# One place more in a ring of raw weights, the residual's rows in a ring of three, and the parts of the output projection in a bound order

## The chip, the cores and the metric

One core of a Trainium2 chip runs the kernel; the other cores are idle. The metric is device time in microseconds (us) of one execution, smaller is better. A measurement's figure is the median of several executions.

## The reference

One layer of a hybrid encoder: 512 rows of `x` and 16 learned meta rows ahead of them, 1024 channels, float32. Two branches (stick-breaking attention and gated linear attention) are merged by gates, go through the output projection `w_o`, and are added to the input through a norm; then comes a gated MLP with a causal convolution. The part around the change is:

```python
mix = (gate_sb * (sb @ w_sb_out[l]) + gate_gla * (o @ w_gla_out[l])) @ w_o[l]
h = h + _rmsnorm(mix, norm_mix_post[l])
hn = _rmsnorm(h, norm_ffn_pre[l])
up = hn @ w_ffn_up[l]
act = gelu(_causal_dwconv(up, conv_w[l], conv_b[l]))
ffn = (act * (hn @ w_ffn_gate[l])) @ w_ffn_down[l]
h = h + _rmsnorm(ffn, norm_ffn_post[l])
return h[:, N_META:]
```

`_rmsnorm` divides each row by the root of its mean square and multiplies by a gain for each channel. `w_sb_out` has 512 rows, `w_o` 1024 x 1024, the up and gate weights 1024 x 2816.

## The kernel before

Products in float32 are made of three matmuls: each operand is split into a high part, rounded to the matmul's type (`h`), and the remainder (`l`), and high x high, high x low and low x high are summed in PSUM. A weight therefore goes through four places: a raw tile in a ring (`raw`, three places, `load_w`, L79), loaded by SyncE's DMA queue (SP); its rounded copy by ScalarE (`wh`, L88); its remainder by GpSimd (`wl`, L89); then TensorE. A raw place is free when both have read it. A framework decides from the code the order in which each engine gets its instructions; `tc.issue_after(x)` binds an instruction behind another one.

The stages by the profile's time: input norm to 20 us, linear attention to 250, stick-breaking and gates to 490, `w_sb_out` and the output projection to 570, the second norm and the first MLP tiles to 605, the MLP's up and gate products to 815, the down projection to the end. The down projection is made of seven products of half-size matrices; some of its operands are sums of two weight blocks, which GpSimd's DMA adds while loading (`tv`, L1115).

The stage of the change works on four tiles of 128 rows (i = 1 to 4) and the two halves of 512 output columns:

- `mix` (L795 to L811): the gated sum for each of eight groups of channels, split into `mh` and `ml`. `w_o`'s second half of columns is loaded into `woh` and `wol` here. For the 16 meta rows, `meta_products` adds small matmuls with the raw weights.
- `second(i)` (L925): the second half of columns for tile i, 24 matmuls of 128 x 512, into the PSUM tile `wob{i}`. `second(1)` and `second(2)` come early, `second(3)` and `second(4)` after the first halves. The dictionary `between` puts other work behind certain matmuls.
- `first_half(i, ks)` (L946): the first half of columns, also 24 matmuls a tile, from the weights `oa0` to `oa6`. Tiles 1 and 2 share one PSUM tile of two banks, `wo12`, tiles 3 and 4 share `wo34`. Groups 0 to 3 go round over all tiles, groups 4 to 7 tile after tile (12 matmuls each, bound behind the last `wob` matmul).
- `gained(i, pt, hf)` (L837): ScalarE sums the squares of a half (`wj`), VectorE multiplies it by the gain `g1bc` into `hb`. It is the last reader of the PSUM half.
- `normed(i)` (L853): the norm's factor (`mix`, `r_mix`, `a_mix`), VectorE's two operations that scale `hb` and add the residual rows `xr`, ScalarE's two squares (`wk`), the next factor (`ffn`, `r_ffn`, `a_ffn`), and two operations that make `y`.
- `turned(i, b)` (L869): four transposes of `y` on TensorE (`ht`) and their split into `h2h`, `h2l`, by ScalarE and VectorE.
- `mini` (L881): norm, residual and second norm of the meta rows, in small operations, from `mc`, a copy of the meta sums; TensorE's part is a packing of 64 small matmuls (`mini`) and two sums (`msmix`, `msffn`). It is a generator that stops twice, so its three steps can be put at three places.
- L967 loads the first two up weights, L976 the first two gate weights; L979 to L986 begin their products.

The residual's 512 rows (`xr`, 2 MB) and the broadcast gains `g1bc` and `g2bc` are loaded on ScalarE's queue at the stage's start (L829 to L833).

Of the kernel before, what the change touches and what calls it, by code (L numbers as in the profile page):

```python
# [9 lines left out]
F32 = mybir.dt.float32  # L10
# [6 lines left out]
P = 128  # L17
D = 1024
# [31 lines left out]
def block_kernel(ctx: ExitStack, tc: tile.TileContext, x, meta_tokens, norm_mix_pre, w_in, w_gk_up, b_gk,  # L50
# [3 lines left out]
    pe, act, dve, pool, sp = nc.tensor, nc.scalar, nc.vector, nc.gpsimd, nc.sync  # L54

    x = x[0]
# [8 lines left out]
    wp = ctx.enter_context(tc.tile_pool(name="wp", bufs=3))  # L65
# [13 lines left out]
    def load_w(src, nk, name, hi_out=None, lo_out=None, lo_eng=pool, into=None):  # L79

        ncol = src.shape[-1]
        raw = wp.tile([P, nk, ncol], F32, tag="raw", name=f"raw_{name}")
        sp.dma_start(raw, src)
        last_raw[0] = raw
        if hi_out is None:
            hi_out = (into or wp).tile([P, nk, ncol], F32R, tag="wh", name=f"wh_{name}", bufs=2)
            lo_out = (into or wp).tile([P, nk, ncol], F32R, tag="wl", name=f"wl_{name}", bufs=2)
        act.copy(hi_out, raw)  # L88
        lo_eng.tensor_tensor(out=lo_out, in0=raw, in1=f32(hi_out), op=ALU.subtract)  # L89
        return hi_out, lo_out  # L90
# [127 lines left out]
    with tc.tile_pool(name="p0", bufs=2, side="right") as p0:  # L218
# [37 lines left out]
        def turned(i, dr):  # L256
            if not i:
                tp = pst("tpm")
                last_tp[0] = pe.matmul(tp[:, :P], xm, dr, start=True, stop=True)
                split_g(p0, hnh[:, :, :NM], hnl[:, :, :NM], tp[:, :P].rearrange("p (t k) -> p k t", k=KT), gT, "m")  # L260
                return
            t = slice(NM + (i - 1) * P, NM + i * P)
            for b in range(2):
                tp = pst(f"tp{i}_{b}", "sz"[i % 2])
                for k in range(4):
                    c = (4 * b + k) * P
                    last_tp[0] = pe.matmul(tp[:, k * P : (k + 1) * P], xts[i][:, c : c + P], dr, start=True, stop=True)
                ks = slice(4 * b, 4 * b + 4)
                low = split_g(p0, hnh[:, ks, t], hnl[:, ks, t], tp.rearrange("p (k t) -> p k t", k=4), gT[:, ks], f"{i}_{b}", LO[i][b])
            return low  # L270
# [515 lines left out]
    meta = pst("meta")  # L786
    pe.matmul(meta, zero[:, :P], zero[:, P:], start=True, stop=False, skip_group_check=True)

    def meta_products(k0, half, raw):
        for kk in range(2):  # L790
            for c in range(2):
                g = 64 * kk + 32 * c
                pe.matmul(meta[g : g + NT, half * 256 : half * 256 + 256], m2[:, k0 + kk, :], raw[:, kk, c * 256 : c * 256 + 256],
                          start=False, stop=False, skip_group_check=True)
# [32 lines left out]
    with tc.tile_pool(name="pw", bufs=1) as pw:  # L827
        g1bc = pw.tile([P, D], F32, name="g1bc")
        act.dma_start(g1bc, norm_mix_post[0].partition_broadcast(P))  # L829
        xr = pw.tile([P, 4, D], F32, name="xr")  # L830
        act.dma_start(xr, x.rearrange("(i p) d -> p i d", p=P))
        g2bc = pw.tile([P, D], F32, name="g2bc")
        act.dma_start(g2bc, norm_ffn_pre[0].partition_broadcast(P))  # L833
        sq = pw.tile([P, 5, 2], F32, name="sq")
        sq2 = pw.tile([P, 5, 2], F32, name="sq2")

        def gained(i, pt, hf):  # L837

            c = slice(hf * 512, hf * 512 + 512)
            pt = pos[(i - 1) // 2][:, (i - 1) % 2 * 512 : (i - 1) % 2 * 512 + 512] if pt is None else pt  # L840
            junk = pw.tile([P, 512], F32, tag="junk", name=f"wj{i}_{hf}")
            act.activation(junk, pt, AF.Square, accum_out=sq[:, i, hf : hf + 1])
            dve.tensor_tensor(out=hb[:, i - 1, c], in0=pt, in1=g1bc[:, c], op=ALU.mult)
# [9 lines left out]

        def normed(i):

            h, xi = hb[:, i - 1, :], xr[:, i - 1, :]
            r = whole(i, sq, "mix")
            for hf in range(2):
                c = slice(hf * 512, hf * 512 + 512)
                dve.scalar_tensor_tensor(out=h[:, c], in0=h[:, c], scalar=r, in1=xi[:, c], op0=ALU.mult, op1=ALU.add)  # L860
                junk = pw.tile([P, 512], F32, tag="junk", name=f"wk{i}_{hf}")
                act.activation(junk, h[:, c], AF.Square, accum_out=sq2[:, i, hf : hf + 1])
            r = whole(i, sq2, "ffn")
            y = ys[i] = pw.tile([P, D], F32, tag="y", name=f"y{i}", bufs=2)
            for b in range(2):
                c = slice(b * 512, b * 512 + 512)
                dve.scalar_tensor_tensor(out=y[:, c], in0=h[:, c], scalar=r, in1=g2bc[:, c], op0=ALU.mult, op1=ALU.mult)
# [54 lines left out]

        last_mm = [None]

        def second(i, between={}):  # L925
            t = (i - 1) * P + NM - T0
            ops = [(m[k][:, t : t + P], w[:, k, :]) for k in range(8) for m, w in ((mh, woh), (mh, wol), (ml, woh))]
            pt = pst(f"wob{i}", "z")
            for q, (a, b) in enumerate(ops):
                last_mm[0] = pe.matmul(pt, a, b, start=q == 0, stop=q == len(ops) - 1)  # L930
                if q in between:
                    between[q]()
            return pt
# [5 lines left out]
        for k in range(0, 8, 2):  # L939
            pairs.append(load_w(wrows(w_o, k, 2, 0, 512), 2, f"oa{k}", into=wx if k > 2 else None))  # L940
            raws.append(last_raw[0])
        meta_products(0, 0, raws[0])
        gained(2, second(2), 1)
        pos = [mmt("wo12"), mmt("wo34")]
# [14 lines left out]
        for i in range(4):  # L959
            with tc.issue_after(last_mm[0].ins):  # L960
                first_half(i, range(4, 8))
            if i == 0:
                meta_products(6, 0, raws[3])
            gained(i + 1, None, 0)
            if i < 2:
                normed(i + 1)
        ups = [load_w(cols(w_up, m * P), KT, f"up{m}") for m in range(2)]  # L967
        mc = pw.tile([P, 512], F32, name="mc")
        act.copy(mc, meta)
        gained(3, second(3, {11: lambda: turned(1, 0), 17: lambda: turned(1, 1)}), 1)  # L970
        normed(3)
        m = mini()
        next(m)
        gained(4, second(4, {5: lambda: turned(2, 0), 11: lambda: turned(2, 1), 17: lambda: next(m)}), 1)
        normed(4)
        gas = [load_w(cols(w_gate, m * P), KT, f"ga{m}", into=wx) for m in range(2)]  # L976

# [1 line left out]
        for m_ in range(2):  # L979
            begun.append(proj(ups[m_], h2h, h2l, FFNS, f"up{m_}", apart=True, only=(0,)))  # L980
            last_mm[0] = last_pr[0]
            turned(3 + m_, 0)
            if m_ == 0:
                next(m)
            pgs_.append(pst(f"ga{m_}", "z"))
            gate_half(pgs_[m_], gas[m_], 0, 256, {11: lambda: turned(3 + m_, 1)})  # L986
        for i in range(4):
# [55 lines left out]
    with tc.tile_pool(name="pd", bufs=1, reuse_waits="tile") as pd:  # L1043
# [12 lines left out]
            return wd[s][:, q : q + nk, c]  # L1056

        def raw_of(s, c, q, nk, nm):
            r = wp.tile([P, nk, HC], F32, tag="raw", name=f"raw_{nm}{q}")
            last_raw[0] = sp.dma_start(r, block(s, c, q, nk))  # L1060
            return r

# [176 lines left out]
```

## Time and profile before

| what | value |
|---|---|
| median of three runs | 947.62 us (947.43 to 950.25) |
| profiled execution, its own time | 947.23 us |
| its span | 945.5 us, so 1.7 us lie around it |
| mean granted clock of TensorE | 0.995 |
| TensorE busy in the span | 920.3 us, 97% |
| VectorE, ScalarE, GpSimd busy | 67%, 52%, 37% |
| DMA, mean over the span | 99 GB/s |

The span is the profiled stretch of one execution. Busy time of TensorE counts matmuls, whose ends are modelled; weight loads beside them are a row of their own (PEld). The list of waits names for each wait of an engine what released it. The granted clock is the share of full speed at which TensorE was allowed to run.

### The profile page before, as it was taken

The numbers are of one execution on the slowest core, as the hardware profiler recorded it, in microseconds if no ns is written. First come the engines' busy times: TensorE is split into PE (matmuls) and PEld (weight loads), VectorE is DVE, ScalarE is ACT, GpSimd is POOL, SyncE is SP. The second block draws the span as 40 slices with busy tenths as digits, with TensorE's granted clock in tenths as the row PEclk, the third lists the DMA queues.
The fourth block names the chain that finished last, engine by engine and source line by source line (L and its number), as shares of the span: only waits on it lengthen the run. The fifth ranks groups of instructions, "written<-read, shape, count | busy, mean of one in ns | idle before, by whom it ended". The sixth has DMA issues, their size and how long they took to land.

```text
span 945.5 us, 17900 instructions
## 1 busy us (share of the span) xinstructions
PE 920.3 (97%) x7229; PEld 842.8 (89%) x7229; DVE 631.7 (67%) x1080; ACT 492.3 (52%) x934; POOL 351.0 (37%) x259
## 2 busy tenths in 40 slices
PE   7999999999999998999999998999999999999996
PEld 7999999999999997999998777999999999988785
DVE  6576858677558785887848438455544445488988
ACT  6674656556567674676663245533333333355654
POOL 5433232333355443554445331544444444101100
PEclk9999999999999999999999999999999999999998
DMA  7122222212223212221214642333333333274923
GB/s 221 46 69 68 69 68 68 68 47 72 64 73 85 62 52 68 67 82 54 73 53 122 232 141 96 101 101 90 89 90 98 102 90 90 90 267 154 266 81 123
DMA packets 129876, 93.39 MB, mean 99 GB/s; under 512 B 4080, under 2 KB 114930, under 8 KB 129794
## 3 DMA queue, kind: packets, MB, share of 16 engines
q1 hardware_dynamic: 126178, 82.55, 29.4%
q10 hardware_dynamic: 2112, 6.82, 2.0%
q0 software_dynamic: 1504, 2.88, 1.8%
q8 instruction: 57, 0.93, 0.4%
q14 instruction: 25, 0.20, 0.1%
HBM read 88.05 MB, written 4.19 MB: 98 GB/s over the span
## 4 chain that ended last, share of the span: by engine, by line
PE 86%; DVE 7%; issue 2%; ACT 2%; POOL 1%; DMA 0%; DVEq 0%; POOLq 0%; ACTq 0%
PE pt_up L113 13%; PE ga L915 12%; PE pt_gv L113 5%; PE pt_gr L113 5%; PE pt_mg L113 4%; PE pt_ms L113 4%; PE pt_go L113 4%; PE dA L1087 3%; PE dD L1087 3%; PE pt_gk L113 3%; PE wob L930 3%; PE pt_so L113 2%; PE pt_gq L113 2%; PE dB L1087 2%; PE wo L951 2%
## 5 line engine op out<-in xcount | busy, mean ns | idle before, releaser
L89 POOL TENSOR_TENSOR wl_ga<-raw_ga,wh_ga 128x1024 fp32r<-128x1024 f32 x22 | 55.3, 2518 | 74.3 <-ACT wh_ga L88 57.1
L89 POOL TENSOR_TENSOR wl_up<-raw_up,wh_up 128x1024 fp32r<-128x1024 f32 x22 | 52.9, 2407 | 79.4 <-ACT wh_up L88 79.4
L113 PE MATMUL pt_up<-h2h,wh_up 128*128 128x256 f32 (+1 forms) x352 | 73.1, 283 | 1.3 <-ACT h2h L140 1.3
L113 PE MATMUL pt_up<-h2l,wh_up 128*128 128x256 f32 (+1 forms) x352 | 73.3, 283 | 0.0
L113 PE MATMUL pt_up<-h2h,wl_up 128*128 128x256 f32 (+1 forms) x352 | 73.2, 282 | 0.0
L915 PE MATMUL ga<-h2h,wh_ga 128*128 128x512 f32 (+1 forms) x192 | 72.0, 376 | 0.7 <-ACT h2h L140 0.7
L915 PE MATMUL ga<-h2l,wh_ga 128*128 128x512 f32 (+1 forms) x192 | 72.1, 376 | 0.0
L915 PE MATMUL ga<-h2h,wl_ga 128*128 128x512 f32 (+1 forms) x192 | 72.1, 376 | 0.0
L88 ACT CAST wh_up<-raw_up 128x1024 fp32r<-128x1024 f32 x22 | 23.1, 1049 | 78.8 <-PE pt_up L113 75.0
L113 PEld LDWEIGHTS pt_up<-h2h,wh_up 128*128 128x128 f32 x352 | 56.8, 189 | 3.3 <-ACT h2h L140 1.6
L113 PEld LDWEIGHTS pt_up<-h2l,wh_up 128*128 128x128 f32 x352 | 55.5, 189 | 0.0
L113 PEld LDWEIGHTS pt_up<-h2h,wl_up 128*128 128x128 f32 x352 | 55.4, 189 | 0.0
L915 PEld LDWEIGHTS ga<-h2h,wl_ga 128*128 128x128 f32 x192 | 36.2, 188 | 7.0
L915 PEld LDWEIGHTS ga<-h2h,wh_ga 128*128 128x128 f32 x192 | 36.1, 188 | 7.0 <-ACT h2h L140 0.9
L915 PEld LDWEIGHTS ga<-h2l,wh_ga 128*128 128x128 f32 x192 | 36.1, 188 | 6.2
L1018 DVE SCALAR_TENSOR_TENSOR cy<-pt_up,cw,cy 128x511 f32<-128x511 f32 (+1 forms) x22 | 16.4, 745 | 36.5 <-ACT cy L1015 36.5
L88 ACT CAST wh_ga<-raw_ga 128x1024 fp32r<-128x1024 f32 x22 | 23.1, 1048 | 26.4 <-PE ga L915 25.2
L1018 DVE SCALAR_TENSOR_TENSOR yp<-pt_up,cw,yp 128x511 f32<-128x511 f32 (+1 forms) x22 | 16.4, 746 | 29.6 <-ACT yp L1015 29.6
L140 ACT CAST sh_p<-As 128x512 fp32r<-128x512 f32 (+1 forms) x30 | 17.4, 584 | 29.4 <-PE dB L1087 12.6
L89 POOL TENSOR_TENSOR wl_gr<-raw_gr,wh_gr 128x1024 fp32r<-128x1024 f32 x8 | 19.1, 2386 | 36.1 <-ACT wh_gr L88 27.2
L1115 POOL DMA_DIRECT2D tv<-in_w_ffn_down_dram x6 | 7.1, 1177 | 68.0 <-DVE wl_p L141 68.0
L113 PE MATMUL pt_gr<-hnh,wh_gr 128*128 128x258 f32 (+1 forms) x128 | 28.2, 294 | 0.0
(558 smaller groups left out, 3170.1 us busy)
## 6 DMA issues: line engine op xcount, KB each, us to landing
raw_up<-in_w_ffn_up_dram SPq DMA_DIRECT2D x22, 512.0 KB, 3.9
raw_ga<-in_w_ffn_gate_dram SPq DMA_DIRECT2D x22, 512.0 KB, 3.8
raw_t<-in_w_ffn_down_dram SPq DMA_DIRECT2D x10, 512.0 KB, 7.4
raw_gv<-in_w_in_dram SPq DMA_DIRECT2D x8, 512.0 KB, 3.9
raw_gr<-in_w_in_dram SPq DMA_DIRECT2D x8, 512.0 KB, 3.8
raw_mg<-in_w_in_dram SPq DMA_DIRECT2D x8, 512.0 KB, 3.8
raw_go<-in_w_gla_out_dram SPq DMA_DIRECT2D x8, 512.0 KB, 4.3
raw_ms<-in_w_in_dram SPq DMA_DIRECT2D x8, 512.0 KB, 4.0
```

The source lines that it names most:

```text
L88: act.copy(hi_out, raw)
L89: lo_eng.tensor_tensor(out=lo_out, in0=raw, in1=f32(hi_out), op=ALU.subtract)
L113: last_pr[0] = pe.matmul(dst, a[:, k, :], b[:, k, lo:hi], start=n == 0, stop=n == len(steps) - 1)
L140: act.copy(hi, src)
L915: last_mm[0] = pe.matmul(pt[:, lo:hi], a[:, k, :], b[:, k, lo:hi], start=lo == 0 and k == 0 and q == 0, stop=k == KT - 1 and q == 2, skip_ ...
L930: last_mm[0] = pe.matmul(pt, a, b, start=q == 0, stop=q == len(ops) - 1)
L951: last_mm[0] = pe.matmul(pos[i // 2][:, (i % 2) * 512 : (i % 2) * 512 + 512], m[k][:, t], w, start=k == 0 and q == 0, stop=k == 7 and q == 2)
L1018: dve.scalar_tensor_tensor(out=y[:, d:], in0=pt[:, : SEQ - d], scalar=c, in1=y[:, d:], op0=ALU.mult, op1=ALU.add)
L1087: mm[i] = pe.matmul(dsts[i], a, b, start=first and k == 0 and j == 0, stop=last and k == NP - 1 and j == 2, skip_group_check=True)
L1115: return lambda n, q, nk: pool.dma_start(out=t[:, q : q + nk, :], in_=block(s, c, q, nk), accum_op=ALU.add)
```

## The change

It has three parts. The ring of raw weights gets a fourth place, in `load_w` and in `raw_of`, the load of the down projection's blocks. The residual's rows are no longer one tile on ScalarE's queue but four, in a ring of three, on SyncE's queue; `g2bc` goes there too. And `second(3)` and `second(4)` are bound as a whole behind the last matmul ahead of them, while `mc` and the steps of `mini` move to earlier places.

```diff
-        raw = wp.tile([P, nk, ncol], F32, tag="raw", name=f"raw_{name}")
+        raw = wp.tile([P, nk, ncol], F32, tag="raw", name=f"raw_{name}", bufs=4)
...
-        xr = pw.tile([P, 4, D], F32, name="xr")
-        act.dma_start(xr, x.rearrange("(i p) d -> p i d", p=P))
         g2bc = pw.tile([P, D], F32, name="g2bc")
-        act.dma_start(g2bc, norm_ffn_pre[0].partition_broadcast(P))
+        xs = {}
+
+        def residual(i):
+            xs[i] = pw.tile([P, D], F32, tag="xr", name=f"xr{i}", bufs=3)
+            sp.dma_start(xs[i], x[(i - 1) * P : i * P, :])
...
-            h, xi = hb[:, i - 1, :], xr[:, i - 1, :]
+            h, xi = hb[:, i - 1, :], xs[i]
...
-        def second(i, between={}):
+        def second(i, between={}, after=None):
...
-                last_mm[0] = pe.matmul(pt, a, b, start=q == 0, stop=q == len(ops) - 1)
+                with tc.issue_after(after.ins) if after else ExitStack():
+                    last_mm[0] = pe.matmul(pt, a, b, start=q == 0, stop=q == len(ops) - 1)
...
+        residual(1)
+        sp.dma_start(g2bc, norm_ffn_pre[0].partition_broadcast(P))
+        residual(2)
...
                 meta_products(6, 0, raws[3])
+                mc = pw.tile([P, 512], F32, name="mc")
+                act.copy(mc, meta)
+            if i == 1:
+                m = mini()
+                with tc.issue_after(last_mm[0].ins):
+                    next(m)
...
-        mc = pw.tile([P, 512], F32, name="mc")
-        act.copy(mc, meta)
-        gained(3, second(3, {11: lambda: turned(1, 0), 17: lambda: turned(1, 1)}), 1)
+        residual(3)
+        residual(4)
+        gained(3, second(3, {2: lambda: next(m), 11: lambda: turned(1, 0), 17: lambda: turned(1, 1)}, last_mm[0]), 1)
         normed(3)
-        m = mini()
-        next(m)
-        gained(4, second(4, {5: lambda: turned(2, 0), 11: lambda: turned(2, 1), 17: lambda: next(m)}), 1)
+        gained(4, second(4, {0: lambda: next(m), 5: lambda: turned(2, 0), 11: lambda: turned(2, 1)}, last_mm[0]), 1)
         normed(4)
...
-            if m_ == 0:
-                next(m)
...
-            r = wp.tile([P, nk, HC], F32, tag="raw", name=f"raw_{nm}{q}")
+            r = wp.tile([P, nk, HC], F32, tag="raw", name=f"raw_{nm}{q}", bufs=4)
```

Lines of the kernel after are up to nine higher than before: L951 becomes L958, L843 becomes L846, L930 becomes L934. In the rows that follow, numbers behind an underscore are buffer numbers, and the bracket names the engines whose work the instruction waits for.

The first place is TensorE's way from the end of tile 1's first half in `wo12` to tile 2's. Before:

```order
L930 MATMUL wob4_7542<-woh_6771,mh2_6901 128x512
L930 MATMUL wob4_7542<-wol_6772,mh2_6901 128x512
L930 MATMUL wob4_7542<-woh_6771,ml2_6902 128x512
L930 MATMUL wob4_7542<-woh_6771,mh3_6940 128x512
L951 MATMUL wo12_7239<-wh_oa4_7197,mh4_6987 128x512 [waits DVE_49]
L951 MATMUL wo12_7239<-wl_oa4_7198,mh4_6987 128x512
```

After:

```order
L958 MATMUL wo12_7241<-wh_oa6_7200,ml6_7074 128x512
L958 MATMUL wo12_7241<-wh_oa6_7200,mh7_7112 128x512
L958 MATMUL wo12_7241<-wl_oa6_7201,mh7_7112 128x512
L958 MATMUL wo12_7241<-wh_oa6_7200,ml7_7113 128x512
L958 MATMUL wo12_7241<-wh_oa4_7194,mh4_6987 128x512 [waits DVE_49]
L958 MATMUL wo12_7241<-wl_oa4_7195,mh4_6987 128x512
```

The waiting matmul had `wob4` (and, further up, `wob3`) ahead of it; now tile 1's own last matmul is directly ahead.

The second place is TensorE's way from tile 3's first half in `wo34` to tile 4's. Before, the end of `wob4` and the mini packing stood ahead of the waiting matmul:

```order
L930 MATMUL wob4_7542<-woh_6771,mh7_7112 128x512
L930 MATMUL wob4_7542<-wol_6772,mh7_7112 128x512
L930 MATMUL wob4_7542<-woh_6771,ml7_7113 128x512
L888 MATMUL mini_7504<-sel_6776,mc_7431 32x2 [waits DVE_49]
L888 MATMUL mini_7504<-sel_6776,mc_7431 32x2 x31
L951 MATMUL wo34_7240<-wh_oa4_7197,mh4_6987 128x512 [waits DVE_49]
```

After, tile 3's own matmuls and one small one, and `wob3` begins behind tile 4's last (the dots leave out the ten matmuls between):

```order
L958 MATMUL wo34_7242<-wl_oa6_7201,mh7_7112 128x512
L958 MATMUL wo34_7242<-wh_oa6_7200,ml7_7113 128x512
L899 MATMUL msmix0_7398<-msqmix0_7396,ones_7150 128x16 [waits Activation_49]
L958 MATMUL wo34_7242<-wh_oa4_7194,mh4_6987 128x512 [waits DVE_49]
L958 MATMUL wo34_7242<-wl_oa4_7195,mh4_6987 128x512
...
L958 MATMUL wo34_7242<-wh_oa6_7200,ml7_7113 128x512
L934 MATMUL wob3_7477<-woh_6771,mh0_6815 128x512
```

So all 48 matmuls of `wob3` and `wob4` have moved from between the first halves to behind them, and the mini packing to between tile 2 and tile 3.

The third place is VectorE, ahead of the operation that frees the first bank of `wo34`, hb<-wo34. Before:

```order
L134 SCALAR_TENSOR_TENSOR a_mix2_7367<-a_mix2_7367,r0_mix2_7362 128x1 [waits DVE_49]
L860 SCALAR_TENSOR_TENSOR hb_7130<-hb_7130,a_mix2_7367,xr_7147 128x512 [waits DVE_49]
L860 SCALAR_TENSOR_TENSOR hb_7130<-hb_7130,a_mix2_7367,xr_7147 128x512
L141 TENSOR_TENSOR h2l_7138<-ht1_0_7446,h2h_7137 128x4x128 [waits Activation_49]
L847 TENSOR_TENSOR ffn2_7376<-sq2_7152 128x1 [waits Activation_49]
L125 TENSOR_SCALAR v_ffn2_7381<-ffn2_7376 128x1 [waits DVE_49]
L141 TENSOR_TENSOR h2l_7138<-ht1_1_7459,h2h_7137 128x4x128 [waits Activation_49]
L843 TENSOR_TENSOR hb_7130<-wo34_7240,g1bc_7145 128x512 [waits Activation_49]
```

After:

```order
L863 SCALAR_TENSOR_TENSOR hb_7130<-hb_7130,a_mix2_7409,xr2_7207 128x512 [waits DMAHW5_49,DVE_49]
L863 SCALAR_TENSOR_TENSOR hb_7130<-hb_7130,a_mix2_7409,xr2_7207 128x512
L132 TENSOR_TENSOR a_mix0_7489<-r0_mix0_7484 128x2 [waits Activation_49]
L133 TENSOR_TENSOR a_mix0_7489<-a_mix0_7489,v_mix0_7487 128x2 [waits DVE_49]
L134 SCALAR_TENSOR_TENSOR a_mix0_7489<-a_mix0_7489,r0_mix0_7484 128x2 [waits DVE_49]
L906 TENSOR_TENSOR hm_7394<-hm_7394,a_mix0_7489 128x16 [waits DVE_49]
L907 TENSOR_TENSOR hm_7394<-hm_7394,mT_98 128x16 [waits DVE_49]
L909 TENSOR_TENSOR hmg_7495<-hm_7394,g2T_97 128x16 [waits DVE_49]
L850 TENSOR_TENSOR ffn2_7418<-sq2_7149 128x1 [waits Activation_49]
L125 TENSOR_SCALAR v_ffn2_7423<-ffn2_7418 128x1 [waits DVE_49]
L846 TENSOR_TENSOR hb_7130<-wo34_7242,g1bc_7145 128x512 [waits Activation_49]
```

The splits of tile 1's transposes (`h2l`) have moved away from there, and the meta rows' small operations have come in. Further up, two rows of `y1` that stood ahead of hb<-wo12 of tile 2 now stand behind it.

On SyncE's queue the loads read, before: oa0, oa2, oa4, oa6, up0, up1, ga0, ga1, up2. After: oa0, oa2, oa4, xr1, g2bc, xr2, xr3, oa6, up0, up1, ga0, ga1, up2, ga2, xr4. In the down projection some loads of raw blocks come one place earlier.

## The prediction

> **What bounds the kernel now.** I read the page first: the busy shares and the chain that ended last.
>
> ```profile
> span 945.5 us, 17900 instructions
> PE 920.3 (97%) x7229; PEld 842.8 (89%) x7229; DVE 631.7 (67%) x1080; ACT 492.3 (52%) x934; POOL 351.0 (37%) x259
> PE 86%; DVE 7%; issue 2%; ACT 2%; POOL 1%; DMA 0%; DVEq 0%; POOLq 0%; ACTq 0%
> ```
>
> TensorE is the bound: 25 us of the span are without it. So a change that leaves its instructions alone, as this one does (it moves them), can be worth only what TensorE waits. Hence the list of its waits (what waited, for what, us in total, times, longest):
>
> ```profile
> PE z L642 <- DVE v0l L145: 2.3, 1, 2.3
> PE ht L876 <- DVE y L867: 1.4, 1, 1.4
> PE pt_up L113 <- ACT h2h L140: 1.3, 1, 1.3
> PE dB L1087 <- DVE sl_p L141: 1.0, 1, 1.0
> PE dD L1087 <- DVE sl_p L141: 0.7, 1, 0.7
> PE ga L915 <- ACT h2h L140: 0.7, 1, 0.7
> PE msmix L896 <- DVE h2l L141: 0.2, 1, 0.2
> ```
>
> No wait names a weight's load, its cast (wh) or its remainder (wl). Four belong to the stage that is rewritten: ht, pt_up, ga and msmix, 1.4 + 1.3 + 0.7 + 0.2 = 3.6 us. I then laid TensorE's timeline of that stage beside the change (start, duration, bracket: idle before it):
>
> ```profile
> 546.80 0.51 PE L951 MATMUL wo<-wh_oa,mh 128*128 128x512 f32 x1
> 547.24 0.61 PE L793 MATMUL meta<-raw_oa,m 128*2 128x256 f32 x8
> 547.78 0.51 PE L930 MATMUL wob<-woh,mh 128*128 128x512 f32 x1
> 552.08 0.40 PE L951 MATMUL wo<-wh_oa,ml 128*128 128x512 f32 x1
> 558.37 0.40 PE L951 MATMUL wo<-wh_oa,mh 128*128 128x512 f32 x1
> 563.96 0.39 PE L930 MATMUL wob<-wol,mh 128*128 128x512 f32 x1
> 568.17 0.71 PE L888 MATMUL mini<-sel,mc 128*32 128x2 f32 x64
> 568.82 0.50 PE L951 MATMUL wo<-wh_oa,mh 128*128 128x512 f32 x1
> ```
>
> Tile 1's first half ends at 552.08; tile 2's, in the other bank of the same PSUM pair wo12, starts at 558.37. In between stand matmuls of wob3 and wob4 alone. The same at wo34: its second bank starts at 568.82, behind ten matmuls of wob4 and the mini packing. The 24 matmuls from 558.37 to 563.96 take 5.59 us, 0.233 each.
>
> **Where the new order puts waits.** In both programs the second bank of a pair waits for VectorE, and VectorE's only reader of the pair is hb<-wo, which scales the first bank. Before, that wait was covered: the reader waits for ScalarE's square wj, and the two and what follows ran beside the wob matmuls between 552.08 and 558.37. Here are those rows of VectorE and ScalarE:
>
> ```profile
> 552.58 0.60 ACT L842 ACTIVATE wj<-wo 128x512 f32<-128x512 f32 x1 [0.59 <-PE wo L951]
> 553.30 0.69 DVE L843 TENSOR_TENSOR hb<-wo,g1bc 128x512 f32<-128x512 f32 x1 [16.67 <-ACT wj L842]
> 557.97 0.19 ACT L862 ACTIVATION_READ_ACCUMULATOR wk<-hb 128x1 f32 x1
> 558.38 0.15 DVE L125 TENSOR_SCALAR v_ffn<-ffn 128x1 f32<-128x1 f32 x1
> 558.95 0.27 DVE L130 TENSOR_SCALAR a_ffn<-v_ffn,r_ffn 128x1 f32<-128x1 f32 x1 [0.41 <-ACT r_ffn L123]
> 559.45 1.41 DVE L867 SCALAR_TENSOR_TENSOR y<-hb,a_ffn,g2bc 128x512 f32<-128x512 f32 x2
> 562.10 0.69 DVE L843 TENSOR_TENSOR hb<-wo,g1bc 128x512 f32<-128x512 f32 x1 [1.23 <-ACT wj L842]
> 563.51 0.27 DVE L130 TENSOR_SCALAR a_mix<-v_mix,r_mix 128x1 f32<-128x1 f32 x1 [0.47 <-ACT r_mix L123]
> 565.52 0.59 ACT L140 CAST h2h<-ht 128x512 fp32r<-128x512 f32 x1
> 566.62 0.58 ACT L140 CAST h2h<-ht 128x512 fp32r<-128x512 f32 x1
> 567.84 0.68 DVE L843 TENSOR_TENSOR hb<-wo,g1bc 128x512 f32<-128x512 f32 x1
> 569.16 0.18 ACT L893 ACTIVATE msqmix<-mini 128x16 f32<-128x16 f32 x1 [0.95 <-DVE hm L902]
> ```
>
> After the change all of wob3 and wob4 stand behind the last matmul of wo34, so no filler is left. I put TensorE at 546.80 at the first row that moves (the same matmul in both programs, with the same rows ahead) and work the new order out.
>
> *First wait.* Twelve wo matmuls (12 x 0.233 = 2.80) and the meta packing (547.24 to 547.78, 0.54) end at 550.14; the last starts at 549.91. wj started 0.50 after the start of the last matmul (552.08, 552.58), and hb<-wo ended 1.41 after wj's start (553.99). So hb<-wo ends at 549.91 + 0.50 + 1.41 = 551.82, and TensorE, whose last modelled end is 550.31, waits **1.5 us**.
>
> *Second wait.* From 551.85: 12 matmuls 2.80, mini 0.65 (568.17 to 568.82), 12 matmuls 2.80, msmix some 0.2: TensorE is ready at 558.3, modelled end 558.5. Then the second bank of wo34 needs hb<-wo of the first. On VectorE and ScalarE that operation now has normed(1), normed(2) and most of mini ahead of it. From wj at 550.41 to the end of tile 1's second square was 5.58 before (552.58 to 558.16), so 555.99; ScalarE's msqmix 0.2 and wj to hb<-wo 0.73 (as 561.37 to 562.10) give 556.9 for tile 2's hb<-wo. From there to hb<-wo of wo34 was 5.74 (562.10 to 567.84). Of that, ScalarE's two h2h casts (0.59 and 0.58, of which 0.9 delayed the squares and wj) go: 4.8. In come on VectorE tile 1's a_ffn (0.5, from 558.95 to 559.45) and y (1.41) and two small operations of mini (0.35, at v_ffn's 0.15 and a gap), less the 0.47 that VectorE idled there for r_mix, so 1.8; on ScalarE msqffn, 0.2. That makes 563.7, and with hb<-wo itself, 0.7, TensorE resumes at 564.4: it waits **5.9 us**. Mini's other six small operations lie beside ScalarE's squares; if they don't, or if some of y does, it is 0.7 more or 0.8 less (5.1 to 6.6).
>
> *What goes.* ht and ga waited at 589 for y4 and for the cast behind it, msmix for a cast. Now 48 wob matmuls (48 x 0.233 = 11.2 us) run while VectorE finishes tiles 1 and 2, and the first up and gate tiles while it finishes 3 and 4; msmix has moved ahead. I take these three waits as gone; if they are not, they cost their 2.3 us again. pt_up still needs the cast of the last transposes of tile 2, which now have six wob4 matmuls ahead: **0.5 us** left of 1.3 (0 to 1.3). So the stage has 1.5 + 5.9 + 0.5 = 7.9 us of waits for 3.6, **+4.3**.
>
> **The clock.** Two waits of before show what one can cost beyond its length, or not:
>
> ```profile
> 359.80 0.78 PE L642 MATMUL z<-v0l,tri 128*128 128x512 f32 x1 [2.27 <-DVE v0l L145]
> 588.95 0.66 PE L876 MATMUL ht<-ident,y 128*128 128x128 f32 x4 [1.36 <-DVE y L867]
> ```
>
> And the windows around them (stretch, length, busy time of PE, PEld, DVE, ACT and POOL, granted clock of TensorE, DMA share, GB/s):
>
> ```profile
> 355.00:360.00 5.00, 1.73 (x10) 1.28 (x10) 4.83 (x6) 0.82 (x4) 3.94 (x4) 0.99 0.37 105
> 360.00:365.00 5.00, 5.00 (x29) 4.91 (x30) 2.28 (x7) 0.60 (x1) 0.53 (x2) 0.67 0.38 105
> 585.00:590.00 5.00, 3.24 (x26) 2.79 (x25) 4.34 (x15) 3.37 (x11) 0.00 (x0) 1.00 0.26 105
> ```
>
> Behind the idle 2.27 us it is 0.67 over five microseconds: 0.33 x 5 = 1.65, with the 0.01 x 5 before it 1.7 us lost. Behind the 1.36 us of 588.95 it stays at 1.00. A wait of 5.9 us is far over the one that fell, so I add **+1.7**; one of 1.5 us is nearest to the one that did not, so nothing for it.
>
> The Trainium skill, TensorE: Matmul & The Clock Gate, Part 1 (What's actually happening), has the clock halve only after a whole idle window of about 3.4 us, in windows that run freely. By that rule a gap of 5.9 us holds a whole window in (5.9 - 3.4) / 3.4, some 7 executions in 10 (an estimate from that page's figure), and the sum would be 951.5 in the other three. The row of 2.27 us is shorter than that window and fell all the same; the measurement decides.
>
> **The other parts.** *The fourth raw place* lets a load start one release earlier; as no wait of TensorE names a load, it removes nothing: 0. Its bounds are set by what it may collide with, in the next two points.
>
> *Residual rows on SyncE's queue.* raw_oa6, up0 and up1 now stand behind three 0.5 MB tiles and g2bc.
>
> ```profile
> 530.02 0.39 ACTq L829 DMA_DIRECT2D g1bc<-in_norm_mix_post_dram  x1
> 530.44 0.45 ACTq L831 DMA_DIRECT2D xr<-in_x_dram  x1
> 544.49 1.05 ACT L88 CAST wh_oa<-raw_oa 128x1024 fp32r<-128x1024 f32 x1 [1.52 <-DMA raw_oa<-in_w_o_dram]
> ```
>
> Before, g1bc, xr (2 MB), g2bc, oa4 and oa6 were 4 MB from 530.0 to 544.5. Now oa4 goes ahead, and g1bc, three tiles, g2bc and oa6 are 3 MB: oa6 lands near 540.9, up1 near 544.5, and the casts end ahead of 549, where TensorE and wj need them: 0, up to 2 us if the three broadcasts and loads share worse.
>
> *Down projection.* The order shows loads of raw_t and of the partial results placed earlier against the accumulating loads of tv, whose readers are close to the end:
>
> ```profile
> L1115 POOL DMA_DIRECT2D tv<-in_w_ffn_down_dram x6: 910/1197/1359, 870.8 to 884.1; - x6
>   ACT wh_p L140: 2.7, 1
> ```
>
> The second row is the longest time that a reader waited for one (ScalarE's cast, 2.7 us): 0 to +2.7; I take 0, as the transfers themselves are the same.
>
> **Sum.** The profiled execution was 947.23 us, 0.4 under the median shown: 947.23 + 4.3 + 1.7 = **953.2**. About 0.3%, 2.8 us, is what a measurement of this kernel tells from no change.
>
> **The rivals.**
> *A, the clock holds or the chain is shorter*: 951.5 and down to 950.2 with a wait of 5.1 and none at pt_up. For it: 2.27 us is one case only. Chance 0.15.
> *B, further loss*: the first wait lowers the clock too (+1.7, 954.9), or the tv loads land late (+2.7, 955.9), or both (957.6). For it: the two waits are only 6.5 us apart. Chance 0.17.
> *C, no change*: VectorE and ScalarE finish their chain sooner, so that the second wait is under 2 us and keeps its clock: 1.5 + 2 + 0.5 - 3.6 gives 947.6. It decides if the chain from wj to hb<-wo of wo34 takes under 10 us where I work out 14.0. Against it: each step has its row. Chance 0.10.
> *D, faster*: the wait of the second bank is met by something older than hb<-wo of the first bank, so that TensorE runs on from one bank to the next. Then both new waits are nothing, the old 3.6 go but for 0.5, and the time is 947.23 - 3.1 = 944.1. It decides where the wait's VectorE operation is: before, 558.37 and 568.82 both lie behind the end of hb<-wo (553.99, 568.52), so the trace does not exclude it. Against it: hb<-wo is the only VectorE operation that reads the pair. Chance 0.06. The Trainium skill, PSUM — Partial Sum Buffer, PSUM bank collisions raise a hardware error, asks for guards by bank and quadrant only; by that rule the two banks need no wait between them, and the time would be that of D. No row here shows a bank running ahead of the other's reader.
>
> **How the numbers follow.** The forecast as worked out (951.6 to 954.8) has 0.52, A 0.15, B 0.17, C 0.10, D 0.06. The range runs from 947.0, which takes in most of C, to 957.0, which takes in B but for its end; D, the rest of C and that end are outside. Faster by over 0.3%: D, 0.06. Within: C and the lowest end of A, 0.14. Slower: 0.80.
>
> **What would show it.** Right: among TensorE's waits two new ones, wo L958 <- DVE hb, near 1.5 and 5.9 us; ht, ga and msmix gone; the granted clock near 0.67 in the five microseconds behind the second; the span's rest shifted by some 6 us and unchanged. Wrong: wo L958 absent from the waits (D); a wait under 2 us (C); the clock at 1.00 behind it (A); new waits of wo for wh_oa or wl_oa, or of dB and dD for wh_p (B, and loads that share worse).

## The result and the profile after

| | median us (range, executions) | ratio to before |
|---|---|---|
| before | 948.13 (947.43 to 950.25, 4) | |
| after | 954.71 (952.40 to 955.14, 4) | 1.006 [1.004, 1.008] |

The change makes the kernel slower by 0.6%, and the forecast of 953.2 was right in sign and 1.5 us low. The profiled execution of after is one of 954.71 us, 7.48 over the profiled one of before (947.23). To see where these 7.48 us lie I took two points that stand outside the stage in both programs: the first matmul of `pt_ms` ahead of it and the first of `dA`, with which the down projection begins, behind it. (In before that is at 828.8 us, and the up and gate products run until then, not only to 815 as in the list of stages.) The groups of these tiles, in before:

```profile
L113 PE MATMUL pt_ms<-hnh,wh_ms x128: 275/282/290, 437.8 to 492.4; 128*128 128x258 f32 x64, 128*128 128x256 f32 x64
L1087 PE MATMUL dA<-wh_p,A x44: 389/395/397, 828.8 to 846.8; 128*128 128x512 f32 x44
```

And in after:

```profile
span 953.0 us, 17915 instructions
L113 PE MATMUL pt_ms<-hnh,wh_ms x128: 275/282/286, 439.2 to 493.8; 128*128 128x258 f32 x64, 128*128 128x256 f32 x64
L1096 PE MATMUL dA<-wh_p,A x44: 389/395/397, 836.1 to 854.1; 128*128 128x512 f32 x44
```

From the one to the other ("the stage's stretch" below) it was 391.0 us and is 396.9: **+5.9**. Ahead of it after is 1.4 us late already (439.2 for 437.8), in code that the change does not touch; that is a step of the first 16 us which other kernels' profiles show too, in code that none of them changes (last section). Behind it the two are alike, 945.5 - 828.8 = 116.7 before and 953.0 - 836.1 = 116.9 after.

TensorE's list of waits has the pair that was forecast; ht, ga and msmix are gone from it (us in total, times, longest):

```profile
PE wo L958 <- DVE hb L846: 6.8, 2, 5.2
PE pt_up L113 <- ACT h2h L140: 0.2, 1, 0.2
```

TensorE's timeline of after shows where they are. The rows of 552.09 and 554.05 are the last matmul of tile 1's first half and the first of tile 2's, in the two banks of `wo12`; 560.55 and 566.04 are the same place at `wo34`:

```profile
552.09 0.40 PE L958 MATMUL wo<-wh_oa,ml 128*128 128x512 f32 x1
554.05 0.50 PE L958 MATMUL wo<-wh_oa,mh 128*128 128x512 f32 x1 [1.56 <-DVE hb L846]
557.03 0.71 PE L891 MATMUL mini<-sel,mc 128*32 128x2 f32 x64
560.55 0.29 PE L899 MATMUL msmix<-msqmix,ones 128*128 128x16 f32 x2
566.04 0.79 PE L958 MATMUL wo<-wh_oa,mh 128*128 128x512 f32 x1 [5.20 <-DVE hb L846]
566.63 0.63 PE L958 MATMUL wo<-wl_oa,mh 128*128 128x512 f32 x1
570.05 0.63 PE L958 MATMUL wo<-wh_oa,mh 128*128 128x512 f32 x1
571.02 0.39 PE L934 MATMUL wob<-woh,mh 128*128 128x512 f32 x1
```

What TensorE waits for is the chain on ScalarE and VectorE, here of after:

```profile
552.58 0.60 ACT L845 ACTIVATE wj<-wo 128x512 f32<-128x512 f32 x1 [0.80 <-PE wo L958]
553.30 0.69 DVE L846 TENSOR_TENSOR hb<-wo,g1bc 128x512 f32<-128x512 f32 x1 [11.31 <-ACT wj L845]
558.81 0.69 DVE L846 TENSOR_TENSOR hb<-wo,g1bc 128x512 f32<-128x512 f32 x1 [0.57 <-ACT wj L845]
559.98 1.41 DVE L870 SCALAR_TENSOR_TENSOR y<-hb,a_ffn,g2bc 128x512 f32<-128x512 f32 x2
563.82 0.63 ACT L865 ACTIVATE wk<-hb 128x512 f32<-128x512 f32 x1 [0.31 <-DVE a_mix L133]
564.58 0.60 ACT L845 ACTIVATE wj<-wo 128x512 f32<-128x512 f32 x1
565.30 0.69 DVE L846 TENSOR_TENSOR hb<-wo,g1bc 128x512 f32<-128x512 f32 x1 [0.37 <-ACT wj L845]
```

Each of the two waits ends where hb<-wo ends (553.99 and 565.99). The one of 565.30 could not start sooner: wj, which it follows, stood behind tile 2's squares (wk) on ScalarE, and those behind tile 1's y and tile 2's residual on VectorE. The windows behind the second wait, where the third number from the right is the granted clock:

```profile
560.00:565.00 5.00, 0.84 (x6) 0.60 (x4) 4.59 (x17) 2.89 (x10) 0.00 (x0) 0.88 0.37 150
565.00:570.00 5.00, 3.96 (x9) 3.14 (x10) 2.46 (x5) 1.60 (x5) 0.00 (x0) 0.50 0.12 48
570.00:575.00 5.00, 5.00 (x24) 4.05 (x23) 0.69 (x1) 2.27 (x5) 4.47 (x2) 0.94 0.21 62
```

The clock is 0.50 in the five microseconds of the restart. From 566.63 to 570.05 eight matmuls take 0.43 us each; 0.233 is what they take elsewhere. Ten such matmuls cost 10 x 0.20 = 2.0 us.

### The profile page after: what moved, and what is told of

Its sections match the earlier page's. It is cut to its first block, busy times and chain, and to the rows that moved or that the text cites. A ratio compares the mean times of both kernels' runs of the same rounds, so it can differ in the third digit from the quotient of the medians.

```text
span 953.0 us, 17915 instructions
## 1 busy us (share of the span) xinstructions
PE 924.6 (97%) x7229; PEld 846.4 (89%) x7229; DVE 632.1 (66%) x1080; ACT 492.8 (52%) x934; POOL 352.3 (37%) x259
## 4 chain that ended last, share of the span: by engine, by line
PE 85%; DVE 7%; issue 3%; ACT 2%; POOL 1%; DMA 1%; SPq 1%; DVEq 0%; ACTq 0%; POOLq 0%
PE pt_up L113 13%; PE ga L918 13%; PE pt_gv L113 5%; PE pt_gr L113 5%; PE pt_mg L113 4%; PE pt_go L113 4%; PE pt_ms L113 3%; PE dA L1096 3%; PE dD L1096 3%; PE pt_gk L113 3%; PE pt_gq L113 2%; PE dB L1096 2%; PE wob L934 2%; PE wo L958 2%; PE pt_sv L113 2%
```

## The experiments

The table lists them all: the median and the ratio beside before on the same chip, and the stage's stretch of the profiled execution, read from the same two groups as above. Medians of before were 947.61 (first four), 947.51 (next four), 948.51 (two) and 947.76 (last two). The names in the first column are those of the parts below. The stretch is that of one execution, and a fall of the clock is worth some 1.7 us in it, so a smaller difference between two stretches says little by itself. Ahead of the stretch the profiles already differ by up to 3.3 us (the first `pt_ms` starts between 437.5 and 440.8), in code that no edit touches (last section). Medians and ratios contain that part, the stretch does not; not bound is the clearest case, with a median 2.9 us above before's, a stretch 0.8 above it, and a `pt_ms` at 440.7.

| kernel | median us (n) | ratio | stage's stretch |
|---|---|---|---|
| before (profile shown) | | | 391.0 |
| after (profile shown) | 954.71 (4) | 1.006 [1.004, 1.008] | 396.9 |
| residual alone | 951.29 (5) | 1.0036 [1.0024, 1.0048] | 394.4 |
| loads alone | 951.48 (5) | 1.0038 [1.0026, 1.0050] | 394.2 |
| order alone | 956.85 (5) | 1.0094 [1.0081, 1.0108] | 399.1 |
| other pairs | 949.68 (9) | 1.0023 [1.0010, 1.0036] | 392.7 |
| not bound | 950.40 (7) | 1.0027 [1.0017, 1.0038] | 391.8 |
| wait filled | 952.39 (6) | 1.0047 [1.0035, 1.0060] | 395.4 |
| pairs, GpSimd held | 948.93 (11) | 1.0009 [1.0000, 1.0017] | 392.2 |
| pairs, not bound | 951.82 (6) | 1.0037 [1.0025, 1.0049] | 393.7 |
| pairs, casts held | 951.78 (6) | 1.0033 [1.0019, 1.0046] | 393.8 |
| pairs, casts held, not bound | 949.79 (11) | 1.0015 [1.0006, 1.0024] | 393.3 |
| pairs, remainder on VectorE | 947.13 (12) | 0.9989 [0.9981, 0.9998] | 389.1 |
| the same, not bound | 946.96 (11) | 0.9991 [0.9983, 1.0000] | 389.1 |

The theory: TensorE loses the time in two waits for hb<-wo, because two tiles that follow each other share one PSUM tile, and in the clock behind the longer one. The rivals: the loads cost it, or the bound order costs it in another way.

### The parts by themselves

**Order alone**: the kernel before with the bound order and the moved mini steps, without the loads' part.

```diff
-        gained(3, second(3, {11: ..., 17: ...}), 1)
+        gained(3, second(3, {2: lambda: next(m), 11: ..., 17: ...}, last_mm[0]), 1)
```

> Before, with the bound order and the moved steps of mini alone; loads as before. If the bound order is the whole loss: 5 to 6 us slower than before, two waits of wo for hb of about 1.5 and 5 us, and the granted clock near 0.5 for three microseconds behind the second. If the loads bring the loss: under 2 us slower.

It is slower than after: 1.0094, and 399.1 us of stretch. The waits stand at the same two places and are longer; TensorE's rows and ScalarE's ahead of the first:

```profile
550.95 1.04 ACT L88 CAST wh_up<-raw_up 128x1024 fp32r<-128x1024 f32 x1 [2.53 <-DMA raw_up<-in_w_ffn_up_dram]
551.90 0.59 ACT L842 ACTIVATE wj<-wo 128x512 f32<-128x512 f32 x1
553.36 0.51 PE L952 MATMUL wo<-wh_oa,mh 128*128 128x512 f32 x1 [2.84 <-DVE hb L843]
566.10 0.79 PE L952 MATMUL wo<-wh_oa,mh 128*128 128x512 f32 x1 [5.92 <-DVE hb L843]
```

The first wait is 1.3 us longer because ScalarE's cast of up1, whose load landed late, stands directly ahead of wj. In after that cast is at 549.24, clear of wj at 552.58. The second wait is 0.7 us longer, and the late up1 is again the likely reason: tile 1's `mix` on VectorE takes 1.23 us for 0.15 in after, and ends at 554.45, when GpSimd's subtraction of up1 does (552.08 + 2.37); in after that subtraction began at 550.37. With the order bound, the loads' part is thus worth some 2 us, most of the 2.2 between the two stretches.

**Residual alone** (before with the residual's rows and `g2bc` on SyncE's queue) and **loads alone** (the same with the fourth raw place). The fourth place alone has no run: beside it the pool of the residual's rows, as before has it, would need 37.1 kB a partition where 33.9 are left, so it is the ring of three that makes room for it.

```diff
-        act.dma_start(xr, x.rearrange("(i p) d -> p i d", p=P))
+            xs[i] = pw.tile([P, D], F32, tag="xr", name=f"xr{i}", bufs=3)
+            sp.dma_start(xs[i], x[(i - 1) * P : i * P, :])
```

> Before, with the residual's rows alone moved to a ring of three on SyncE's queue; three raw places and the old order of the output projection stay. If the bound order is the whole loss: same as before, within 1 us, no wait of TensorE on a cast of oa6 or up. If the loads bring a part of it: slower by 1 to 2 us, with a wait of wo for wh_oa or wl_oa.

> The changed kernel with the old order of the output projection: fourth raw place and residual ring stay, so the two parts of the change that are loads. If the bound order is the whole loss: same as before, within 1 us, and the old waits (ht, pt_up, ga, some 3.6 us) are back. If the fourth place disturbs the start of the kernel, where the changed kernel's profile stood 1.4 us later: slower by 1 to 2 us in most executions.

Both cost 3.2 to 3.4 us of stretch, and no wait names a load or its cast. The order of TensorE has become another one: the mini packing, one piece before, is cut in two around tile 4's first half. In residual alone:

```profile
570.41 0.43 PE L891 MATMUL mini<-sel,mc 128*32 128x2 f32 x30
573.75 0.48 PE L891 MATMUL mini<-sel,mc 128*32 128x2 f32 x34
576.19 0.66 PE L879 MATMUL ht<-ident,y 128*128 128x128 f32 x4 [1.38 <-ACT msqmix L896]
578.98 0.61 PE L899 MATMUL msmix<-msqmix,ones 128*128 128x16 f32 x2 [1.69 <-DVE v_mix L125]
```

```profile
575.00:580.00 5.00, 2.12 (x11) 1.86 (x12) 4.12 (x9) 2.87 (x9) 3.31 (x2) 0.79 0.41 117
580.00:585.00 5.00, 5.00 (x26) 5.00 (x26) 4.28 (x18) 3.15 (x12) 0.00 (x0) 0.53 0.57 197
```

Its two waits, 1.4 + 1.7 = 3.1 us, are no more than the 3.6 of before. But they stand within 3 us of each other, and the clock falls behind them: (1 - 0.79) x 5 + (1 - 0.53) x 5 = 3.4 us, which is all of the loss. Loads alone shows the same: mini cut in two (42 and 22 matmuls), waits of ht (0.9) and msmix (1.6) close together, and 3.4 us lost to the clock. So the loads by themselves do cost, it seems through the order that the framework then chooses. No run holds the old order with the new loads, but not bound, below, comes near: it has these loads and the earlier steps of mini, its mini packing is one piece, the clock holds, and the stretch is only 0.8 over before. The parts do not add: +8.1 for the order and +3.2 for the loads, +5.9 for both.

### The shared PSUM tile and the binding

**Other pairs**: after, with tiles 1 and 3 in one PSUM tile and 2 and 4 in the other, so that tiles that follow each other share none.

```diff
-        pos = [mmt("wo12"), mmt("wo34")]
+        pos = [mmt("wo13"), mmt("wo24")]
...
-                    last_mm[0] = pe.matmul(pos[i // 2][:, (i % 2) * 512 : ...
+                    last_mm[0] = pe.matmul(pos[i % 2][:, (i // 2) * 512 : ...
```

> The changed kernel, but tiles 1 and 3 share one PSUM pair and tiles 2 and 4 the other, so that neighbours in the order no longer share a pair; nothing else. If the two waits come from the shared pair: the first wait is gone, the second is under 1.5 us and leaves the clock at full, 7 to 8 us faster than the changed kernel, so about 946.5, at or under before. If the waits are VectorE being late in any case: no change, 953 to 955.

The two waits of 6.8 us become one of 0.2: the shared tile is shown to be their cause. The stretch falls from 396.9 to 392.7, but not to before's 391.0, since a new wait has come for the cast of tile 2's transposes, with a fall of the clock behind it. TensorE's rows and the window of the fall:

```profile
560.90 0.50 PE L958 MATMUL wo<-wh_oa,mh 128*128 128x512 f32 x1 [0.22 <-DVE hb L846]
579.51 0.39 PE L113 MATMUL pt_up<-h2h,wh_up 128*128 128x256 f32 x1 [2.40 <-ACT h2h L140]
```

```profile
580.00:585.00 5.00, 4.89 (x29) 4.77 (x28) 4.79 (x14) 1.76 (x8) 0.00 (x0) 0.66 0.00 0
```

VectorE is late there, and its rows and GpSimd's suggest why; the last pair of runs below tests it. The two residual operations of tile 2, 1.41 us in after, take 3.57, and a multiplication of 16 columns, 0.17 in after, takes 2.37, while GpSimd subtracts the gate weights:

```profile
563.44 3.57 DVE L863 SCALAR_TENSOR_TENSOR hb<-hb,a_mix,xr 128x512 f32<-128x512 f32 x2
566.93 2.37 DVE L906 TENSOR_TENSOR hm<-hm,a_mix 128x16 f32<-128x16 f32 x1
563.76 5.50 POOL L89 TENSOR_TENSOR wl_ga<-raw_ga,wh_ga 128x1024 fp32r<-128x1024 f32 x2 [10.26 <-ACT wh_ga L88]
```

With the waits gone, TensorE frees the weights' places sooner, and ScalarE's cast and GpSimd's subtraction of the gate weights, which start on that, move (from 569.05 and 570.17 in after to 562.64 and 563.76, though this profile is 1.5 us later ahead of the stage) into VectorE's busiest stretch.

**Not bound**: after, with the bound order taken back and the rest kept.

```diff
-        gained(4, second(4, {0: ..., 5: ..., 11: ...}, last_mm[0]), 1)
+        gained(4, second(4, {0: ..., 5: ..., 11: ...}), 1)
```

> The changed kernel with the binding of the second halves taken away; loads and the earlier steps of mini stay. If the binding makes the two waits: wob matmuls stand between the first halves again, both waits of wo for hb are under 0.5 us, the clock holds there, and the old waits at the first up tile come back: 948 to 951. If the moved steps of mini make them: still 953 or more.

No wo waits any more either. What is left in the stage is smaller, and the longest of TensorE's waits there are:

```profile
PE ht L879 <- DVE h2l L141: 1.4, 1, 1.4
PE pt_up L113 <- DVE h2l L141: 1.1, 1, 1.1
```

The clock is at 1.00 behind them, and the stretch is 391.8, 5.1 less than after. So it is the binding, with shared tiles, that costs.

### The clock

**Wait filled**: after, with twenty 128 x 512 matmuls more between tile 3's and tile 4's first halves, into a PSUM tile that nobody reads.

```diff
+            if i == 2:
+                idle = pst("idle", "z")
+                for q in range(20):
+                    with tc.issue_after(last_mm[0].ins):
+                        last_mm[0] = pe.matmul(idle, mh[0][:, :P], woh[:, 0, :], start=True, stop=True)
```

> The changed kernel with 20 more matmuls of 128 x 512, whose result nobody reads, put into its second wait (20 x 0.233 = 4.7 of 5.2 us). If the clock falls because TensorE idles there: granted clock 1.00 behind it, the next twelve matmuls 0.233 apart instead of 0.43, and 1.7 to 2.0 us faster than the changed kernel although it does more work. If the clock has nothing to do with the wait: no faster, or slower by what doesn't fit.

```profile
552.75 0.50 PE L958 MATMUL wo<-wh_oa,mh 128*128 128x512 f32 x1 [1.56 <-DVE hb L846]
559.25 4.84 PE L981 MATMUL idle<-woh,mh 128*128 128x512 f32 x20
565.28 0.49 PE L958 MATMUL wo<-wh_oa,mh 128*128 128x512 f32 x1 [1.06 <-DVE hb L846]
```

```profile
565.00:570.00 5.00, 4.72 (x20) 3.87 (x21) 3.34 (x12) 2.79 (x5) 1.86 (x1) 1.00 0.00 0
```

TensorE works through most of the wait and the clock stays at 1.00 behind it; matmuls that produce nothing make the stretch 1.5 us shorter than after's (395.4 for 396.9). The clock's share is thus shown apart from the wait's: the 2.0 us come back, less the 0.5 by which tile 4 starts later behind tile 2 than in after (565.28 - 552.75 = 12.53 for 566.04 - 554.05 = 11.99).

### What other pairs still lose

**Pairs, GpSimd held**: other pairs, with the subtraction of the gate weights bound behind tile 2's y.

```diff
+        with tc.issue_after(lo_after.ins) if lo_after else ExitStack():
+            lo_eng.tensor_tensor(out=lo_out, in0=raw, in1=f32(hi_out), op=ALU.subtract)
```

> The kernel with the other pairs, and GpSimd's remainders of the two gate weights held back until y of tile 2 is done. If its 2.4 us wait at the first up tile comes from VectorE's residual operation taking 3.6 instead of 1.4 us beside GpSimd: that operation is back at 1.4 us, the wait under 0.8 us, the clock holds, and it is 3 to 4 us faster than with the other pairs alone, near 946. If the wait comes from ScalarE's order (tile 3's squares ahead of the cast): no faster, 949 to 950.

The binding had no effect: GpSimd began at 560.72, although tile 2's y on VectorE, behind which its instruction is bound, begins only at 570.16. So here the binding made no engine wait for another. GpSimd's row is as long as in other pairs, and pt_up waits 2.4 us again:

```profile
560.72 5.51 POOL L90 TENSOR_TENSOR wl_ga<-raw_ga,wh_ga 128x1024 fp32r<-128x1024 f32 x2 [10.28 <-ACT wh_ga L88]
```

It is in effect a second measurement of other pairs.

**Pairs, not bound**: the same without the bound order.

> The kernel before this one in the list, with the binding of the second halves taken away too. If fillers between the first halves are worth more than the cover they give later: 944 to 946 with no wait over 1 us in the stage. If the cover at the first up tile is worth more: a wait of pt_up or ht of 1 to 2.5 us comes back, and 946 to 949.

Slower than either alone: ht waits 1.9 us for y, pt_up 1.1 for h2l, and the clock is 0.66 in 580 to 585.

**Pairs, casts held**: other pairs, with ScalarE's casts of the gate weights (ahead of which GpSimd cannot begin) bound behind tile 2's last factor on ScalarE, and **the same, not bound**.

```diff
+        with tc.issue_after(hi_after.ins) if hi_after else ExitStack():
+            act.copy(hi_out, raw)
...
+                held = last_exp[0]
```

> The kernel with the other pairs, and ScalarE's casts of the two gate weights held behind tile 2's last norm factor on ScalarE itself, so that GpSimd's remainders start later. If VectorE's residual operation of tile 2 was long because of GpSimd: 1.4 us instead of 3.6, the wait at the first up tile from 2.4 to about 1 us, the clock holds there, 3 us faster than with the other pairs alone, near 946 and at or under before. If ScalarE's order alone makes that wait: the operation is short, the wait and the time stay (949).

> As the one before, with the binding of the second halves taken away too. If the binding still costs: the best of all, 944 to 946. If the cover that it leaves for the transposes of tile 2 is worth more: waits of ht for y or h2l of 1 to 2 us, and 1 to 3 us slower than the one before.

The gain did not come. The residual of tile 2 is back at 1.41 us, but GpSimd's subtraction, now at 568.06, meets tile 2's y, and pt_up waits longer still:

```profile
568.09 5.71 DVE L871 SCALAR_TENSOR_TENSOR y<-hb,a_ffn,g2bc 128x512 f32<-128x512 f32 x2
579.29 0.39 PE L114 MATMUL pt_up<-h2h,wh_up 128*128 128x256 f32 x1 [3.25 <-ACT h2h L141]
```

The collision was moved, not removed. Without the bound order y is 3.55 and hm 2.38, and ht waits for mssffn and v_mix (1.5 and 0.9).

**Pairs, remainder on VectorE**: casts held as before, and VectorE itself makes the two remainders, behind tile 2's y; and **the same, not bound**.

```diff
-        gas = [load_w(..., hi_after=held) for m in range(2)]
+        gas = [load_w(..., lo_eng=dve, hi_after=held, lo_after=last_y[2]) for m in range(2)]
```

> Other pairs and casts held as before, and the two remainders of the first gate weights are made by VectorE behind tile 2's y instead of by GpSimd. Theory (what the other pairs still lose is VectorE's work stretched beside GpSimd's subtraction): y of tile 2 back at 1.4 us for the two (5.71 with the casts held), the two remainders 1.2 to 1.4 us each on VectorE right behind it, no GpSimd row there; pt_up's wait falls from 3.25 to under 1 us, the clock behind it stays at 1.00; 951.8 less 2.6 of wait and 1.7 of clock, 947.5, some 1.0 under the kernel before of the same chip. Rival (the bound order alone makes VectorE late, whoever subtracts): pt_up still waits over 2.4 us with the clock at 0.66 behind it, 951 or more.

> The same with second(3) and second(4) not bound. Theory: against the kernel with other pairs, unbound and casts held (949.8), y of tile 2 falls from 3.55 to 1.4 us and hm from 2.38 to 0.2, the two waits of ht (1.5 and 0.9) fall under 1 us together, the clock in 575 to 585 is 1.00; 949.8 less 1.5 of wait and 2.0 of clock: 946.3. Rival: the waits of ht stay, as they come of the meta rows' chain (mssffn, v_mix) and not of the collision: 949 or more.

VectorE's rows, TensorE's and the window that fell before, of the bound one:

```profile
567.98 1.42 DVE L872 SCALAR_TENSOR_TENSOR y<-hb,a_ffn,g2bc 128x512 f32<-128x512 f32 x2
569.31 2.35 DVE L91 TENSOR_TENSOR wl_ga<-raw_ga,wh_ga 128x1024 fp32r<-128x1024 f32 x2
575.79 0.39 PE L115 MATMUL pt_up<-h2h,wh_up 128*128 128x256 f32 x1 [0.24 <-ACT h2h L142]
```

```profile
580.00:585.00 5.00, 5.00 (x45) 5.00 (x44) 4.05 (x10) 2.75 (x9) 0.00 (x0) 1.00 0.24 93
```

The two y operations are back at 1.42 us, and VectorE does in 2.35 us what took GpSimd 5.2 beside it. pt_up waits 0.5 us in total for 3.5, the clock stays at 1.00, and the stretch is 389.1 us, 7.8 under after and 1.9 under before. Measured, that is 0.9989 [0.9981, 0.9998] of before: with the shared tile and the collision gone, the bound order costs nothing, and the whole is about 0.1% faster than before, less than the 0.3% that I take as a difference. Its profile lost 1.7 us to the clock near 255 us, which before's did not (last section). Without the binding the stretch is 389.1 too: there the binding makes no difference either way. The remainder on VectorE was not tried in the kernel before, so whether the 1.9 us come from the change at all or from that move is open.

## Why the prediction was right, point by point

- **First wait**: 1.5 forecast, 1.56 measured. By the chain as written: last matmul, wj 0.5 us behind its start, hb<-wo.
- **Second wait**: 5.9 forecast, 5.20 measured. TensorE was ready 0.2 us later than worked out, and the chain from wj (552.58) to the end of hb<-wo of wo34 (565.99) took 13.4 us instead of 14.0: 0.3 less up to tile 2's hb<-wo (558.81), 0.3 less from there. That is near the lower end of 5.1 to 6.6, and near A's 5.1.
- **pt_up**: 0.5 forecast, 0.2 measured. ht, ga and msmix gone, as forecast (msmix had waited for `h2l`, VectorE's split, not for a cast; nothing hung on it).
- **The clock**: 1.7 forecast, 2.0 measured. The place was right; the size was taken from a fall of 1.7 us in all, and this one was of 0.12 x 5 + 0.50 x 5 + 0.06 x 5 = 3.4 in the three windows, of which the part ahead of 566.04 fell into the wait itself. So the fall was twice as large as the one that it was taken from (0.50 in the five microseconds behind the wait, not 0.67), and that its cost came out close is luck.
- **Sum of the stage**: 4.3 + 1.7 = 6.0 forecast; 1.56 + 5.20 + 0.2 + 2.0 - 3.6 = 5.4 by the rows, 5.9 by the stretch. Of the 0.5 between the two, 0.3 is a wait of the meta products for m that after has and before has not; the rest is not settled. That forecast and stretch agree to 0.1 is in part luck: the second wait and pt_up were 1.0 us shorter than forecast, the clock and what the sum does not contain made up for it.
- **Down projection**: 0 forecast; 116.7 and 116.9 us from dA's first matmul to the end. The bound of 2.7 us was misread: that row is ScalarE's cast waiting for VectorE's sum `tw`, and the list of waits has for the tv loads themselves, in before, only VectorE's 0.8 us. In after VectorE waits 1.4 and ScalarE 0.2 for them, but TensorE's waits there are the same (dB 1.0, dD 0.7).
- **Loads**: 0 forecast, right in this kernel and for a reason that I had not seen. oa6 landed at 543.7, not at 540.9, as its load was issued late, and no wait of TensorE came of it; up1's cast came clear of wj, which is worth 1.3 us at the first wait with the bound order. Alone the loads cost 3.2 to 3.4 us. The step "as no wait of TensorE names a load, it removes nothing" counted transfers only, and left out that the framework may order TensorE anew around them.
- **The rivals**: D is refuted in this form: the wait is for the whole PSUM tile of two banks, and goes when consecutive tiles share none. The rule of guards by bank and quadrant (the Trainium skill, PSUM — Partial Sum Buffer, PSUM bank collisions raise a hardware error) does not foretell this wait: its 5.20 us were for a reader of the other bank. Whether the chip would have needed it was not tried. C needed a chain under 10 us and had 13.4. Of A, the shorter chain came nearly (5.20), but the clock did not hold. Of B, the first wait left the clock at 1.00, and TensorE waited no longer behind the tv loads.
- **The 1.4 us over the sum** in the profiled execution come from the first 16 us, not from the change.

## What to carry to other kernels

To the waits of this kernel, two banks of one PSUM tile are one thing. Before work is bound into a row, look what stood between the last matmul into the one bank and the first into the other, as it was the cover of the reader's chain. A stall that is taken away releases the buffers behind it sooner; ask which engine starts on that and whom it meets. And where a change of loads alone costs and no wait names a load, read the new order of the other engines, which may have changed with it.

## What the runs showed of the hardware that was not expected

- **VectorE stood still beside GpSimd's subtraction.** An operation on 16 columns took 2.37 us for 0.17, about as long as one subtraction of 128 x 1024 (2.40 in after), and two operations of y took 5.71 for 1.41. In order alone hb<-wo, of whose two large operands one is in PSUM, took its usual 0.69 us (552.62) inside such a subtraction, and `mix`, right behind it, stood until its end. The Trainium skill, SBUF — State Buffer, Terms, has the two share a port pair that one holds for a whole instruction while the other blocks; these rows agree.
- **The clock falls by something other than the length of one wait.** In the stage it fell behind 2.40 and 3.25 us and behind a pair of 1.38 and 1.69, and stayed at 1.00 behind the 2.84 us of order alone. Behind the wait of 2.27 us at 360 it fell in all 14 profiles. Near 255, behind a wait of zs of 0.89 or 0.90 us that all 14 have, it fell in six and held in eight. In before and in pairs, casts held:

```profile
255.00:260.00 5.00, 4.86 (x41) 4.69 (x42) 1.69 (x7) 3.47 (x9) 2.83 (x3) 1.00 0.00 0
255.00:260.00 5.00, 4.86 (x28) 4.64 (x29) 0.86 (x3) 2.68 (x7) 2.37 (x1) 0.66 0.00 0
```

The fall, summed over the windows, came in two sizes: 1.7 us (behind 2.40: 0.34 x 5) and 3.4 (after, residual alone); behind the 2.27 it was 1.7 in before and 3.4 in loads alone (0.23 x 5 + 0.46 x 5). The Trainium skill, TensorE: Matmul & The Clock Gate, Part 1 (What's actually happening), has windows of some 3.4 us; half speed for one or two of them would lose 1.7 or 3.4 us (an estimate from that page's figure), which are just these sizes. But a whole idle window, which that section asks for, was not needed.
- **The same code starts in two ways.** The first 16 transposes of TensorE, the same code in all 14 profiles, take 2.05 us in eight of them and 3.78 in six, of before and of after here:

```profile
7.14 2.05 PE L267 MATMUL tp<-drin,xt 128*128 128x128 f32 x16 [0.89 <-DVE drin L215]
```

```profile
7.08 3.78 PE L267 MATMUL tp<-drin,xt 128*128 128x128 f32 x16 [0.43 <-DVE drin L215]
```

In after everything behind is 1.4 us later, though the windows give the clock as 1.00 in both. This step and the fall near 255 together make most of the differences ahead of the stage: a first `pt_ms` at 437.8 with neither (before), 439.2 with the slow start (after), 439.4 with the fall (pairs, casts held), 440.7 with both (not bound). Before's 14 executions beside the first experiments fall into two groups, eight from 946.83 to 947.72 and six from 948.30 to 949.24; that one such step separates them fits its size and is not shown. Differences of this size between two profiles are no effect of an edit until the parts ahead of it have been compared.
